# Gate and up of three feed-forwards as seven products of block sums, in an fp32 decoder trunk on one Trainium2 core

## The chip, the cores and the metric

The kernel runs on one core of one Trainium2 chip. The metric is the device time of one execution in microseconds (us), the median of the runs. The engines of the core have names in this text as in the profile: PE is TensorE's matmuls, PEld its loads of the stationary operand, DVE is VectorE, ACT is ScalarE, POOL is GpSimd, SP is SyncE, which here only issues DMAs.

## The reference, cut to what matters

```python
def rms_norm(x, g):
    y = x32 * lax.rsqrt(jnp.mean(x32 * x32, axis=-1, keepdims=True) + NORM_EPS)
    return y * g

def swiglu(x, w_gate, w_up, w_down):
    return (jax.nn.silu(x @ w_gate) * (x @ w_up)) @ w_down

def reference(x, positions, ...):          # x (1, 512, 2048), D_FF = 1536, DEPTH = 2, all float32
    h = x
    for i in range(DEPTH):
        h = h + 0.5 * swiglu(rms_norm(h, norm_g[i, 0]), ffn_w_gate[i, 0], ffn_w_up[i, 0], ffn_w_down[i, 0])
        hn = rms_norm(h, norm_g[i, 1])
        mix = even_mixer(hn, ...) if i % 2 == 0 else odd_mixer(hn, ...)   # attention; pooling and stick-breaking
        h = h + mix
        h = h + 0.5 * swiglu(rms_norm(h, norm_g[i, 2]), ffn_w_gate[i, 1], ffn_w_up[i, 1], ffn_w_down[i, 1])
    return rms_norm(h, final_norm)
```

There are four feed-forwards of 512 positions, 2048 features and 1536 hidden features, and two mixers with their projections between them.

## The kernel before, in words

The activations lie transposed, features on the 128 partitions and the 512 positions along the row: `xg[k]`, k = 0 to 15, is 128 features of all positions. So that fp32 products keep their accuracy, each operand is split in two parts: a high part written as fp32r by an ACT copy, and the rest, `src - high`, by a DVE subtraction. A product of two such pairs is three matmuls (`mm3`: high by high, high by low, low by high) into one PSUM bank. The norm's factor per position, `norm.R`, is multiplied onto the result; its gain is put into `xg` beforehand.

A feed-forward (`ffn`) goes over 12 blocks of 128 hidden features. For each it sums gate into one PSUM bank and up into another, over all 16 k, 48 matmuls each; there the weights' 128 x 128 blocks are stationary and 512 positions move. Then come `gate` (DVE multiply, ACT Silu), `up` (two DVE multiplies) and the split of the result into `hid[f]`. The down projection goes over 16 blocks `d` of 128 output features, 12 k each, 36 matmuls; DVE adds half of it to the residual `x`, and a sink splits the new `x` with the next norm's gain into the next `xg`, squares it on ACT (`Norm.add`, line 329) and adds the square on POOL (line 333). The last down projection does its last four blocks in two halves of positions.

The weights come as a stream of chunks in the order in which PE takes them (`weight_plan`). A chunk is up to 1024 columns of 128 partitions, 512 KB. `load_to` gives the DMA on SP's queue (line 212) into one of 3 raw buffers, `split_to` gives the ACT copy (line 223) and the DVE subtraction (line 224) into one of 3 pairs `wh`, `wl`, and `chunk` does both ahead of the matmuls that use them. The schedule is the order of the program: each engine takes its instructions in the order in which the code gives them, and waits at each for what it needs. Work beside the main stream (heads of attention, rope tables, the last norm) consists of generators in `side`; each call of `tick` gives one more step of one of them.

The norm's sums are closed at the start of the stage that follows, in `Norm.stages`: 4 tiny matmuls with a column of ones (`nps`), a DVE step, a power on POOL, and then, where `bc` is set, 4 transposes (`npb`) that spread the factor over the partitions for `norm.R`. `out_part` is the output projection of a mixer, in two parts by heads, and has the same sink. Residuals of the second and third feed-forward stay in SBUF; around the mixers they are written to DRAM and read back (`spill`, `reload`).

Of the kernel before, what the change touches and what calls it, by code (L numbers as in the profile page):

```python
# [16 lines left out]
P = 128  # L17
S = 512
# [22 lines left out]
DOWN = ((0, NK, 0, S),)  # L41
LAST_DOWN = ((0, NK - 4, 0, S), (NK - 4, NK, 0, S // 2), (NK - 4, NK, S // 2, S))
NRAW = 3
NSPL = 3

# ---------------------------------------------------------------- the order of the weights
# [7 lines left out]
def weight_plan():  # L54
    """(source, layer, half, k0, k1, [(c0, c1), ...]) of each chunk, as TensorE takes them."""
    plan = []
# [8 lines left out]
    def ffn(i, j, first=False, last=False):  # L65
# [10 lines left out]
        for d0, d1, _, _ in LAST_DOWN if last else DOWN:  # L76
            for d in range(d0, d1):
                cols("ffn_w_down", i, j, halves(NF), d * P, d * P + P)
# [18 lines left out]
    for d in range(NK):  # L97
        cols("even_w_out", 0, 0, ((0, A_H),), d * P, d * P + P)
    for d in range(0, NK, 2):
        cols("even_w_out", 0, 0, ((A_H, A_H + B_H),), d * P, d * P + 2 * P)  # L100
    ffn(0, 1)
    ffn(1, 0)
# [9 lines left out]
    for part in range(2):  # L112
        for d in range(0, NK, 2):
            cols("odd_w_out", 0, 0, ((4 * part, 4 * part + 4),), d * P, d * P + 2 * P)
    ffn(1, 1, last=True)
    return plan
# [14 lines left out]
def shape_constants():  # L131
    """Tables that depend on the shapes alone."""
# [38 lines left out]
def trunk(ctx: ExitStack, tc: tile.TileContext, xT, pos_row, pos_col, wts, gains, consts, bias_a_in, bias_b_in, outT):  # L171
    nc = tc.nc
    plan = weight_plan()
# [29 lines left out]
    # ------------------------------------------------------------ the stream of weights  # L203
    nxt_load, nxt_split, nxt_use = [0], [0], [0]
    raw_t, split_t = {}, {}

# [8 lines left out]

    def split_to(i):
        while nxt_split[0] <= min(i, len(plan) - 1):
            j = nxt_split[0]
            n = offsets[j][1]
            r = raw_t.pop(j)  # L220
            h = spl.tile([P, 1024], F32R, tag="wh", name=f"wh_{j}")
            low = spl.tile([P, 1024], F32R, tag="wl", name=f"wl_{j}")
            nc.scalar.activation(h[:, :n], r[:, :n], AF.Copy)  # L223
            nc.vector.tensor_tensor(low[:, :n], r[:, :n], f32(h[:, :n]), op=ALU.subtract)  # L224
            split_t[j] = (h, low)
            nxt_split[0] += 1

    def ahead(i):
        """What may be fetched and split once the products of the chunk before the i-th are given."""
        load_to(i + NRAW + 1)  # L230
        split_to(i + NSPL - 1)

    def chunk(name):
        i = nxt_use[0]
        nxt_use[0] += 1
        assert plan[i][0] == name, (i, plan[i], name)
        ahead(i)
        h, low = split_t.pop(i)
        kk = plan[i][4] - plan[i][3]
        n = offsets[i][1]  # L240
        view = lambda t: t[:, :n].rearrange("p (k c) -> p k c", k=kk)
        return view(h), view(low), range(plan[i][3], plan[i][4])
# [6 lines left out]
    def split(src, s, scale=None, cols=None, late=None):  # L249
        """src (times a column) as two parts of 12 bits; the second one, if late is a list, when its entry is called."""  # L250
# [15 lines left out]
    # ------------------------------------------------------------ work beside the main stream  # L266
# [19 lines left out]
    # ------------------------------------------------------------ constants  # L286
# [123 lines left out]
    # ------------------------------------------------------------ feed-forward  # L410
    def ffn(xg, norm, resid_in, sink, first=False, down=DOWN, beside=None):
# [3 lines left out]
        def half_of(ps, name):  # L415
            wh, wl, ks = chunk(name)
            for i, k in enumerate(ks):
                mm3(ps, wh[:, i, :], wl[:, i, :], xg[k][0], xg[k][1], k == 0, k == NK - 1)
# [14 lines left out]
        if first:  # L433
            pss = [bank("gu") for _ in range(4)]
            for i in range(NK):
                half_of(pss[i % 4], ("ffn_w_gate", "ffn_w_up")[i % 2])
# [26 lines left out]
        for d0, d1, c0, c1 in down:  # L463
            for d in range(d0, d1):
                pd = bank("pd")[:, :c1 - c0]
                for _ in range(2):
                    wh, wl, ks = chunk("ffn_w_down")
                    for i, k in enumerate(ks):
                        mm3(pd, wh[:, i, :], wl[:, i, :], hid[k][0][:, c0:c1], hid[k][1][:, c0:c1], k == 0, k == NF - 1)
                    tick()  # L470
                x = resid_in(d)[:, c0:c1]
                nc.vector.scalar_tensor_tensor(x, pd, 0.5, x, op0=ALU.mult, op1=ALU.add)
                sink(d, x, slice(c0, c1))

    def make_sink(gain, norm, xg, spill=None, keep=None):
        late = []

        def sink(d, x, cols):
# [3 lines left out]
            if d == NK - 1:  # L482
                late.pop()()
            norm.add(x)
            if spill is not None:
                nc.scalar.dma_start(spill[d], x)
            if keep is not None:
                keep[d] = x
# [6 lines left out]
    # ------------------------------------------------------------ attention  # L495
    # Softmax: query blocks; keys and probabilities of blocks in three tiles.
# [4 lines left out]
    def softmax_head(qk, v, bias, scale, merged):  # L501
        """One head: q and k of [features, positions], v of key blocks; the result in merged."""
# [39 lines left out]
    # Stick-breaking: keys on partitions, their queries along the rows, key blocks in three tiles.  # L542
# [65 lines left out]
    # ------------------------------------------------------------ projections  # L608
    def project(name, xg):
        """128 columns of a projection, transposed."""  # L610
        ps = bank("pj")
        for _ in range(2):
            wh, wl, ks = chunk(name)
            for i, k in enumerate(ks):
                mm3(ps, wh[:, i, :], wl[:, i, :], xg[k][0], xg[k][1], k == 0, k == NK - 1)
# [3 lines left out]
    def project_rows(name, xs_of, n, n_chunks, k_last):  # L619
# [352 lines left out]
```

## Time and profile before

| | |
|---|---|
| median of 3 runs | 2329.05 us (2328.59 to 2329.12) |
| span of the profiled execution, first to last instruction | 2327.4 us |
| PE busy | 2307.6 us, 99% of the span |
| DVE, ACT, POOL busy | 1031.5, 769.9, 200.0 us |
| mean granted clock of TensorE | 0.998 of full speed |
| moved by DMA | 243.85 MB, 105 GB/s over the span |

The profile holds the span of its execution and no other time of it; the runs' median is 1.65 us above that span, which is taken as what lies around it. The stages by the profile's time: first feed-forward to 402 us, even mixer with its output to 837, second feed-forward to 1230, third to 1623, odd mixer with its output to 1915, fourth to 2312, last norm to 2327. A matmul's duration in the trace (389 ns) is longer than its distance from the next one, because matmuls overlap; the distance is what counts for time.

### The profile page before, as it was taken

To read this page: it belongs to the slowest core of one execution; us is meant where nothing else is said; L and a number is where in the kernel's file an instruction comes from. 1 tells how busy PE (TensorE), PEld (TensorE's weight loads), DVE (VectorE), ACT (ScalarE), POOL (GpSimd) and SP (SyncE) were. 2 spreads that over 40 slices of the span, in tenths; PEclk is the share of its full clock that TensorE was granted. 3 is DMA by queue.
4 is the path that set the end of the run, shared out by engine and by line. 5 is a ranking of instruction groups with operands and counts; after the bars stand their busy time and mean duration, and the time that the engine had idled before them with its cause. 6 is when DMAs were issued, how large, how long until landed. Compare 5 with 4: busy or idle time off the path is not lost.

```text
span 2327.4 us, 26261 instructions
## 1 busy us (share of the span) xinstructions
PE 2307.6 (99%) x10640; PEld 1937.8 (83%) x10640; DVE 1031.5 (44%) x1350; ACT 769.9 (33%) x1086; POOL 200.0 (9%) x194
## 2 busy tenths in 40 slices
PE   9999999999999999999999999999999999999997
PEld 7888888989888888888888888888888888888887
DVE  4443344464645653333443333344435664333335
ACT  5322233232334442222332222233235553222233
POOL 3000011000011130000110000011300030000013
PEclk9999999999999999999999999999999999999999
DMA  6232334322223332332333332334322422222224
GB/s 210 91 100 91 98 127 136 102 72 97 82 81 128 105 100 91 100 99 82 100 101 98 100 100 91 97 127 138 100 96 82 145 91 100 100 91 100 89 95 161
DMA packets 83530, 243.85 MB, mean 105 GB/s; under 512 B 9296, under 2 KB 13520, under 8 KB 83408
## 3 DMA queue, kind: packets, MB, share of 16 engines
q1 hardware_dynamic: 73328, 224.23, 29.7%
q10 hardware_dynamic: 10080, 17.94, 2.2%
q8 instruction: 83, 1.36, 0.2%
q14 instruction: 39, 0.32, 0.0%
HBM read 229.55 MB, written 12.58 MB: 104 GB/s over the span
## 4 chain that ended last, share of the span: by engine, by line
PE 98%; DVE 0%; DMA 0%; ACT 0%; issue 0%; POOL 0%; DVEq 0%; SPq 0%; ACTq 0%; POOLq 0%
PE pd L246 7%; PE pd L247 7%; PE pd L245 7%; PE pu L245 7%; PE pu L247 7%; PE pg L245 7%; PE pg L247 7%; PE pu L246 7%; PE pg L246 7%; PE pj L245 5%; PE pj L247 5%; PE pj L246 5%; PE wo L245 3%; PE wo L247 3%; PE wo L246 3%; PE pr L245 2%
## 5 line engine op out<-in xcount | busy, mean ns | idle before, releaser
L224 DVE TENSOR_TENSOR wl<-raw,wh 128x1024 fp32r<-128x1024 f32 (+3 forms) x463 | 549.9, 1189 | 755.4 <-ACT wh L223 754.4
L223 ACT ACTIVATE wh<-raw 128x1024 fp32r<-128x1024 f32 (+3 forms) x463 | 443.7, 960 | 609.9 <-issue 185.2
L333 POOL TENSOR_TENSOR sq<-sq,sq 128x512 f32<-128x512 f32 (+1 forms) x110 | 145.4, 1322 | 1916.9 <-ACT sq L329 1915.8
L247 PE MATMUL pd<-hidh,wl 128*128 128x512 f32 (+1 forms) x816 | 307.3, 377 | 0.3 <-DVE wl L224 0.3
L245 PE MATMUL pd<-hidh,wh 128*128 128x512 f32 (+1 forms) x816 | 307.4, 377 | 0.0
L246 PE MATMUL pd<-hidl,wh 128*128 128x512 f32 (+1 forms) x816 | 307.2, 377 | 0.0
L245 PE MATMUL pu<-xgh,wh 128*128 128x512 f32 x736 | 287.0, 390 | 0.0
L245 PE MATMUL pg<-xgh,wh 128*128 128x512 f32 x736 | 286.4, 389 | 0.0
L247 PE MATMUL pu<-xgh,wl 128*128 128x512 f32 x736 | 286.4, 389 | 0.0
L246 PE MATMUL pu<-xgl,wh 128*128 128x512 f32 x736 | 286.4, 389 | 0.0
L247 PE MATMUL pg<-xgh,wl 128*128 128x512 f32 x736 | 286.3, 389 | 0.0
L246 PE MATMUL pg<-xgl,wh 128*128 128x512 f32 x736 | 286.3, 389 | 0.0
L245 PE MATMUL pj<-xgh,wh 128*128 128x512 f32 x464 | 181.7, 392 | 0.0
L247 PE MATMUL pj<-xgh,wl 128*128 128x512 f32 x464 | 180.8, 390 | 0.0
L246 PE MATMUL pj<-xgl,wh 128*128 128x512 f32 x464 | 180.7, 389 | 0.0
L247 PEld LDWEIGHTS pd<-hidh,wl 128*128 128x128 f32 x816 | 153.5, 188 | 28.5 <-DVE wl L224 0.5
L245 PEld LDWEIGHTS pd<-hidh,wh 128*128 128x128 f32 x816 | 153.6, 188 | 28.1
L246 PEld LDWEIGHTS pd<-hidl,wh 128*128 128x128 f32 x816 | 153.6, 188 | 28.1
L247 PEld LDWEIGHTS pu<-xgh,wl 128*128 128x128 f32 x736 | 138.2, 188 | 28.8
L247 PEld LDWEIGHTS pg<-xgh,wl 128*128 128x128 f32 x736 | 138.2, 188 | 28.7
L246 PEld LDWEIGHTS pg<-xgl,wh 128*128 128x128 f32 x736 | 138.2, 188 | 28.7
L246 PEld LDWEIGHTS pu<-xgl,wh 128*128 128x128 f32 x736 | 138.2, 188 | 28.6
(215 smaller groups left out, 2721.1 us busy)
## 6 DMA issues: line engine op xcount, KB each, us to landing
raw<-wts SPq DMA_DIRECT2D x275, 512.0 KB, 3.4
raw<-wts SPq DMA_DIRECT2D x161, 384.0 KB, 3.0
spill<-x ACTq DMA_DIRECT2D x32, 256.0 KB, 2.0
x<-spill ACTq DMA_DIRECT2D x32, 256.0 KB, 2.9
raw<-wts SPq DMA_DIRECT2D x18, 256.0 KB, 2.9
x<-xT SPq DMA_DIRECT2D x16, 256.0 KB, 4.7
outT<-sc SPq DMA_DIRECT2D x16, 256.0 KB, 2.4
raw<-wts SPq DMA_DIRECT2D x8, 416.0 KB, 3.0
```

The costliest lines, as they stand in the source:

```text
L223: nc.scalar.activation(h[:, :n], r[:, :n], AF.Copy)
L224: nc.vector.tensor_tensor(low[:, :n], r[:, :n], f32(h[:, :n]), op=ALU.subtract)
L245: nc.tensor.matmul(out, ah, bh, start=start, stop=False)
L246: nc.tensor.matmul(out, ah, bl, start=False, stop=False)
L247: nc.tensor.matmul(out, al, bh, start=False, stop=stop)
L333: nc.gpsimd.tensor_tensor(self.accs[0], self.accs[0], sq, op=ALU.add)
```

## The change

The second, third and fourth feed-forward compute gate and up by another algorithm (`ffn_products`); the first one, the down projections and the mixers keep theirs.

The 2048 features are two halves (k below and from 8), the 512 positions two halves (256 each), and gate and up of one block of weights are the two columns of a 2 x 2 block matrix. Instead of eight products of blocks there are seven, of sums of blocks (Winograd's form of Strassen's algorithm). Of the inputs, B11, B21, B22 and four sums T1 to T4 are made once per feed-forward and k (`Pieces`): four DVE subtractions of 256 columns and the splits of seven pieces of 256 columns. Of the weights, four sums per block are made in place in the raw buffers by DVE. The products are by position blocks: a 128 x 128 block of a piece is stationary, and 512 hidden features of the weights move. So one unit of 512 hidden features takes 7 products x 8 k x 2 position blocks x 3 matmuls = 336, and 3 units make 1008, beside 1152 before. Units run in two phases, P1, P2 and P4 first (6 PSUM banks), then P6, P5, P7, P3 (8 banks); the results are combined by DVE adds, Silu takes the norm's factor as its scale, and the hidden values, now positions on partitions, are transposed on PE, 16 blocks per unit, and split (`to_hidden`).

For this the stream of weights has a second plan, `uses`: raw chunks of up to 1024 columns in 6 buffers, and splits of at most 512 columns into 4 pairs, everywhere in the kernel. A block of 2 k x 512 columns that is in two products is loaded twice. All sinks write the new residual to DRAM, and the blocks `d` are taken in pairs d, d + 8. The first 5 k of the next pieces are made in `side`, the other three when unit 0 first needs them.

```diff
-NBLK = 81
-NRAW = 3
-NSPL = 3
+NBLK = 79
+NRAW = 6
+NSPL = 4
+LATER = 5
...
+    def ffn_products(i, j, down):              # in the plan of the weights
+        for u in range(FF // UNIT):
+            c0, c1 = u * UNIT, (u + 1) * UNIT
+            blk = lambda name, k: plan.append((name, i, j, k, k + 2, ((c0, c1),)))
+            for k in range(0, HK, 2):
+                blk("ffn_w_up", k)
+                blk("ffn_w_up", HK + k)
+                blk("ffn_w_gate", HK + k)
+            whole()
+            for k in range(0, HK, 2):
+                r = len(plan)
+                a22, a21, a11, a12 = r, r + 1, r + 2, r + 3
+                blk("ffn_w_gate", HK + k)
+                blk("ffn_w_gate", k)
+                blk("ffn_w_up", k)
+                blk("ffn_w_up", HK + k)
+                uses[-3][3].append((a22, a21, 1, a22))
+                uses[-2][3].append((a21, a11, -1, a21))
+                for a, sums in ((a11, [(a11, a22, -1, a11)]), (a22, []), (a21, []), (a12, [(a12, a12, -1, a11)])):
+                    uses.append((a, 0, 1, sums))
+                    uses.append((a, 1, 2, []))
...
     def split_to(i):
-        while nxt_split[0] <= min(i, len(plan) - 1):
+        while nxt_split[0] <= min(i, len(uses) - 1):
             j = nxt_split[0]
+            r, k0, k1, sums = uses[j]
+            load_free()
+            for to, a, sign, b in sums:
+                n = offsets[to][1]
+                nc.vector.tensor_tensor(raw_t[to][:, :n], raw_t[a][:, :n], raw_t[b][:, :n],
+                                        op=ALU.add if sign > 0 else ALU.subtract)
...
+            nc.scalar.activation(h[:, :n], src, AF.Copy)
+            nc.vector.tensor_tensor(low[:, :n], src, f32(h[:, :n]), op=ALU.subtract)
...
+    def take(name, n):
+        while n:
+            i = nxt_use[0]
+            nxt_use[0] += 1
+            r, k0, k1, _ = uses[i]
+            ahead(i)                            # split_to(i + NSPL - 1)
...
+        def steps(self, k, b1, b2):             # Pieces
+            t12, t34 = blk("t12"), blk("t34")
+            sub(t12[:, lo], b1[:, hi], b1[:, lo])
+            sub(t34[:, lo], b2[:, hi], b1[:, hi])
+            sub(t12[:, hi], b2[:, hi], t12[:, lo])
+            sub(t34[:, hi], b2[:, lo], t12[:, hi])
+            yield
+            b = blk("pb", F32R)
+            nc.scalar.activation(b[:, lo], b1[:, lo], AF.Copy)
+            nc.vector.tensor_tensor(b[:, hi], b1[:, lo], f32(b[:, lo]), op=ALU.subtract)
+            b2h, b2l = split(b2, "pb")
+            yield
+            t12h, t12l = split(t12, "pt")
+            yield
+            t34h, t34l = split(t34, "pt")
...
+        def product(names, piece, ps, kc):
+            for k, wh, wl in take(names, 2):
+                k %= HK
+                sh, sl = pieces.get(k)[piece]
+                for a in range(2):
+                    c = slice(a * P, a * P + P)
+                    mm3(ps[a], sh[:, c], sl[:, c], wh, wl, k == 0, k == HK - 1)
...
+        for u in range(FF // UNIT):
+            p1, p2, p4 = ([bank("pa") for _ in both] for _ in range(3))
+            for kc in range(HK // 2):
+                if u == 0 and kc < last:
+                    pieces.get(2 * kc + 2), pieces.get(2 * kc + 3)
+                product("ffn_w_up", "B11", p1, kc)
+                ...                             # kc == last: s1 = copy of p1 (ACT); u == 0, kc < 2: next(ng)
+                tick()
+                product("ffn_w_up", "B21", p2, kc)
+                ...                             # kc == last: c11 = p2 + s1
+                tick()
+                product("ffn_w_gate", "T4", p4, kc)
+                ...                             # kc == last: s4 = copy of p4 (ACT)
+                tick()
+            p6, p5, p7, p3 = ([bank("pb") for _ in both] for _ in range(4))
+            for kc in range(HK // 2):
+                product("ffn_w_up", "T2", p6, kc)
+                if kc == last:
+                    for a in both:
+                        nc.vector.tensor_tensor(s1[a], p6[a], s1[a], op=ALU.add)
+                        nc.vector.tensor_tensor(s4[a], s4[a], s1[a], op=ALU.add)
+                tick()
+                product("ffn_w_gate", "T1", p5, kc)
+                if kc == last:
+                    for a in both:
+                        nc.vector.tensor_tensor(s1[a], p5[a], s1[a], op=ALU.add)
+                tick()
+                product("ffn_w_gate", "T3", p7, kc)
+                if kc == last:
+                    c22 = [blk("c22") for _ in both]
+                    for a in both:
+                        nc.vector.tensor_tensor(s4[a], p7[a], s4[a], op=ALU.add)
+                        nc.scalar.activation(s4[a], s4[a], AF.Silu, scale=norm.r[:, a:a + 1])
+                        nc.vector.tensor_tensor(c22[a], p7[a], s1[a], op=ALU.add)
+                        nc.scalar.activation(c22[a], c22[a], AF.Silu, scale=norm.r[:, 2 + a:3 + a])
+                        nc.vector.scalar_tensor_tensor(c11[a], c11[a], norm.r[:, a:a + 1], s4[a], op0=ALU.mult,
+                                                       op1=ALU.mult)
+                tick()
+                product("ffn_w_up", "B22", p3, kc)
+                tick()
+            for a in both:
+                nc.vector.tensor_tensor(s1[a], p3[a], s1[a], op=ALU.add)
+                nc.vector.scalar_tensor_tensor(s1[a], s1[a], norm.r[:, 2 + a:3 + a], c22[a], op0=ALU.mult, op1=ALU.mult)
+            side.append(to_hidden(u, c11 + s1))
...
+    def piece_sink(gain, norm, pieces, spill):
+        def sink(d, x, cols):
+            b = blk("xb")
+            nc.scalar.activation(b, x, AF.Copy, scale=gain(d))
+            held.append(b)
+            if d >= HK:
+                pieces.add(d - HK, *held)
+                held.clear()
+            norm.add(x)
+            nc.scalar.dma_start(spill[d], x)
```

## Rows read from the trace of the kernel before

**Rows 1.** The page: busy time, chain that ended last, DMA issues (KB, us to landing).
```profile
PE 2307.6 (99%) x10640; PEld 1937.8 (83%) x10640; DVE 1031.5 (44%) x1350; ACT 769.9 (33%) x1086; POOL 200.0 (9%) x194
...
PE 98%; DVE 0%; DMA 0%; ACT 0%; issue 0%; POOL 0%; DVEq 0%; SPq 0%; ACTq 0%; POOLq 0%
...
x<-xT SPq DMA_DIRECT2D x16, 256.0 KB, 4.7
```

**Rows 2.** Stretches (busy us per engine, clock, DMA share, GB/s): start, second feed-forward, end.
```profile
0.00:58.00 58.00, 52.19 (x217) 42.57 (x218) 27.44 (x39) 33.53 (x54) 20.77 (x19) 1.00 0.63 211
...
843.00:1236.00 393.00, 393.00 (x1741) 325.54 (x1740) 154.78 (x165) 113.09 (x141) 23.12 (x18) 1.00 0.31 97
...
2316.00:2327.40 11.40, 0.00 (x0) 0.00 (x0) 6.23 (x5) 0.00 (x0) 5.09 (x4) 0.50 0.66 226
```

**Rows 3.** Timeline of PE and ACT (start us, duration) in the second feed-forward's gate.
```profile
903.97 0.39 PE L245 MATMUL pg<-xgh,wh 128*128 128x512 f32 x1
...
914.39 0.39 PE L246 MATMUL pg<-xgl,wh 128*128 128x512 f32 x1
...
914.85 0.39 PE L245 MATMUL pu<-xgh,wh 128*128 128x512 f32 x1
914.87 1.06 ACT L223 ACTIVATE wh<-raw 128x1024 fp32r<-128x1024 f32 x1 [4.38 <-PE pg L246]
```

**Rows 4.** One tile's matmuls in the odd mixer, where inputs are stationary and weights move.
```profile
L245 PE MATMUL pr<-wh,xgh x9: 389/389/389, 1668.4 to 1673.8; 128*128 128x512 f32 x9
```

**Rows 5.** The chain in order of time (start, us): transposes.
```profile
471.56 1.09 PE pt L528 x10
...
854.70 0.44 PE npb L350 x4
```

**Rows 6.** Timeline of DVE and ACT around one hidden block, second feed-forward.
```profile
904.24 0.69 DVE L428 TENSOR_TENSOR up<-pu,R 128x512 f32<-128x512 f32 x1 [3.37 <-PE pu L247]
...
904.96 0.69 DVE L429 TENSOR_TENSOR gate<-gate,up 128x512 f32<-128x512 f32 x1
...
905.75 0.63 ACT L255 ACTIVATE hidh<-gate 128x512 fp32r<-128x512 f32 x1 [6.14 <-DVE gate L429]
...
906.29 1.05 ACT L223 ACTIVATE wh<-raw 128x1024 fp32r<-128x1024 f32 x1
...
906.49 0.69 DVE L256 TENSOR_TENSOR hidl<-gate,hidh 128x512 fp32r<-128x512 f32 x1 [0.83 <-ACT hidh L255]
```

**Rows 7.** Timeline of DVE, operations one behind the other.
```profile
832.10 0.68 DVE L647 TENSOR_TENSOR x<-wo,x 128x512 f32<-128x512 f32 x1
832.70 0.74 DVE L259 SCALAR_TENSOR_TENSOR xgl<-x,gn,xgh 128x512 fp32r<-128x512 f32 x1
...
1713.80 1.23 DVE L224 TENSOR_TENSOR wl<-raw,wh 128x1024 fp32r<-128x1024 f32 x1 [0.19 <-ACT wh L223]
1714.94 2.72 DVE L259 SCALAR_TENSOR_TENSOR mgcl<-mx,gn,mgch 128x512 fp32r<-128x512 f32 x4
```

**Rows 8.** DMA issues of 512 KB (KB each, median us to landing): second feed-forward's gate and up.
```profile
raw<-wts SPq DMA_DIRECT2D x28, 512.0 KB, 3.6
```

**Rows 9.** Timeline of DVE and POOL at the even mixer's output.
```profile
840.33 3.02 POOL L333 TENSOR_TENSOR sq<-sq,sq 128x512 f32<-128x512 f32 x2 [3.11 <-ACT sq L329]
...
842.43 2.00 DVE L224 TENSOR_TENSOR wl<-raw,wh 128x1024 fp32r<-128x1024 f32 x1 [1.60 <-ACT wh L223]
```

**Rows 10.** The chain in order of time (start, us) at the kernel's start.
```profile
11.23 0.43 PE gu L247
...
12.07 0.24 PE gu L246
```

**Rows 11.** Timeline of PE and POOL after a down projection (third feed-forward starts at 1230.37).
```profile
1230.37 0.39 PE L245 MATMUL pg<-xgh,wh 128*128 128x512 f32 x1
...
1232.74 1.36 POOL L333 TENSOR_TENSOR sq<-sq,sq 128x512 f32<-128x512 f32 x1 [6.87 <-ACT sq L329]
```

**Rows 12.** Timeline of DVE in the softmax of one head, even mixer.
```profile
496.12 0.18 DVE L520 RECIPROCAL rden<-den 128x4 f32<-128x4 f32 x1 [2.36 <-ACT pr L518]
```

More of the change, by code (lines that the diff above doesn't have):

```diff
@@ L54, in weight_plan, with plan_and_uses, whole @@
 def weight_plan():
-    plan = []
+    return plan_and_uses()[0]
+def plan_and_uses():
+    plan, uses = [], []
+    def whole():
+        for r in range(uses[-1][0] + 1 if uses else 0, len(plan)):
+            _, _, _, k0, k1, cs = plan[r]
+            w = sum(b - a for a, b in cs)
+            parts = -(-(k1 - k0) * w // 512)
+            step = -(-(k1 - k0) // parts)
+            for k in range(0, k1 - k0, step):
+                uses.append((r, k, min(k + step, k1 - k0), []))
     def cols(name, i, j, ks, c0, c1):
@@ L63, in halves, with ffn @@
         return ((0, n // 2), (n // 2, n))
-    def ffn(i, j, first=False, last=False):
+    def ffn_products(i, j, down):
[19 more added lines that the diff above has]
+                    uses.append((a, 1, 2, []))
+        for n, (d, _, _) in enumerate(down):
+            if n == 0:
+                for k0, k1 in ((0, 8), (8, NF)):
+                    for e in (down[0][0], down[1][0]):
+                        plan.append(("ffn_w_down", i, j, k0, k1, ((e * P, e * P + P),)))
+            elif n > 1:
+                cols("ffn_w_down", i, j, ((0, 8), (8, NF)), d * P, d * P + P)
+    def ffn(i, j, first=False):
         f = 0
@@ L96, in weight_plan @@
     plan.append(("even_w_kv_up", 0, 0, 0, 2, tuple((h * kvh + NOPE, (h + 1) * kvh) for h in range(B_H))))
[L97 to L102, printed above, removed]
+    for ks in ((0, A_H), (A_H, A_H + B_H)):
+        for d in PAIRS:
+            cols("even_w_out", 0, 0, (ks,), d * P, d * P + P)
+    whole()
+    ffn_products(0, 1, PAIR_DOWN)
+    whole()
+    ffn_products(1, 0, PAIR_DOWN)
     for g in range(4):
@@ L112, in weight_plan @@
     for part in range(2):
[L113 to L116, printed above, removed]
+        for d in PAIRS:
+            cols("odd_w_out", 0, 0, ((4 * part, 4 * part + 4),), d * P, d * P + P)
+    whole()
+    ffn_products(1, 1, LAST_DOWN)
+    whole()
+    return plan, uses
 def plan_offsets(plan):
@@ L205, in trunk @@
     raw_t, split_t = {}, {}
+    last_split = {}
+    for n, (r, _, _, sums) in enumerate(uses):
+        last_split.update({c: n for c in (r, *(x for t, a, _, b in sums for x in (t, a, b)))})
     def load_to(i):
@@ L408, in rope_tables, with ffn, half_of @@
         rope_b["cos"], rope_b["sin"] = cb, sb
-    def ffn(xg, norm, resid_in, sink, first=False, down=DOWN, beside=None):
+    def ffn(xg, norm, resid_in, sink, first=False, beside=None):
         hid = {}
         ng = norm.stages() if norm is not None else None
[L415 to L418, printed above, removed]
+        def half_of(ps, name, n=HK):
+            for k, wh, wl in take(name, n):
+                mm3(ps, wh, wl, xg[k][0], xg[k][1], k == 0, k == NK - 1)
         def gate(ps):
@@ L462, in ffn @@
             tick()
[L463 to L473, printed above, removed]
@@ L475, in make_sink, with down_half, down_done @@
-    def make_sink(gain, norm, xg, spill=None, keep=None):
+        for job in DOWN:
+            pd = bank("pd")
+            for _ in range(2):
+                down_half(pd, job, hid, NF // 2)
+                tick()
+            down_done(pd, job, resid_in, sink)
+    def down_half(pd, job, hid, n):
+        _, c0, c1 = job
+        for k, wh, wl in take("ffn_w_down", n):
+            mm3(pd[:, :c1 - c0], wh, wl, hid[k][0][:, c0:c1], hid[k][1][:, c0:c1], k == 0, k == NF - 1)
+    def down_done(pd, job, resid_in, sink):
+        d, c0, c1 = job
+        x = resid_in(d)[:, c0:c1]
+        nc.vector.scalar_tensor_tensor(x, pd[:, :c1 - c0], 0.5, x, op0=ALU.mult, op1=ALU.add)
+        sink(d, x, slice(c0, c1))
@@ new lines, in trunk, with __init__, add, get @@
+    class Pieces:
+        def __init__(self):
+            self.of, self.work = {}, {}
+        def add(self, k, b1, b2):
+            g = self.steps(k, b1, b2)
+            self.work[k] = g
+            if k < LATER:
+                side.append(g)
+        def steps(self, k, b1, b2):
+            t12, t34 = blk("t12"), blk("t34")
+            lo, hi = slice(0, H), slice(H, S)
+            sub = lambda o, a, b: nc.vector.tensor_tensor(o, a, b, op=ALU.subtract)
+            sub(t12[:, lo], b1[:, hi], b1[:, lo])
[11 more added lines that the diff above has]
+            t34h, t34l = split(t34, "pt")
+            self.of[k] = {
+                "B11": (b[:, lo], b[:, hi]), "B21": (b2h[:, lo], b2l[:, lo]), "B22": (b2h[:, hi], b2l[:, hi]),
+                "T1": (t12h[:, lo], t12l[:, lo]), "T2": (t12h[:, hi], t12l[:, hi]),
+                "T3": (t34h[:, lo], t34l[:, lo]), "T4": (t34h[:, hi], t34l[:, hi])}
+        def get(self, k):
+            if k not in self.of:
+                finish(self.work[k])
+            return self.of[k]
@@ L476, in make_sink @@
+    def make_sink(gain, norm, xg, spill):
         late = []
@@ L703, in trunk @@
     side.append(rope_tables())
-    ffn(xg, norm, lambda d: xs[d], make_sink(g_norm(1), norm1, xg1, spill=spill0), first=True, beside=started)
+    ffn(xg, norm, lambda d: xs[d], make_sink(g_norm(1), norm1, xg1, spill0), first=True, beside=started)
     xs.clear()
```

215 lines of the change are left out of this document (127 added, 88 removed).

## The prediction

> **What bounds the kernel now.** Read the page first: PE is busy 99% of the span, and the chain that ended last is 98% PE [rows 1]. The stretches say that this holds inside a stage too: the second feed-forward has PE busy for 393.0 of 393 us at full clock, DVE 155, ACT 113, DMA share 0.31 [rows 2]. So the time is the number of matmuls times their distance. The timeline gives the distance: 48 matmuls from 903.97 to 914.85, 226.7 ns each [rows 3]. With weights moving and inputs stationary it is the same: nine of every third matmul from 1668.4 to 1673.8, 24 distances in 5.4 us, 225 ns [rows 4]. What leaves PE's stream therefore leaves the time, as long as the engines that feed PE keep up; and they get more to do.
>
> **PE's own account.** Removed: 1152 - 1008 = 144 matmuls in each of three feed-forwards, 432 x 0.2267 = 97.9 us; and the four norm transposes of three norms, 3 x 0.44 = 1.3 [rows 5]. Added: 3 x 48 transposes of 128 x 128; ten took 1.09 us [rows 5], so 144 x 0.109 = 15.7. Without one stall the span would be 2327.4 - 97.9 - 1.3 + 15.7 = 2243.9. No stall at all is the lower end of every term below; the question is how much DVE gives back.
>
> **DVE's prices.** Independent operations of 512 columns follow each other at 0.60 us (832.10 to 832.70, busy 0.68), and 1024 columns take 1.14 (1713.80 to 1714.94) [rows 7]; the line through both gives 256 columns 0.33, an estimate. An operation that reads what the one before it wrote follows after 0.72 (904.24 to 904.96) [rows 6]. A subtraction that waits for an ACT copy of what DVE has just written starts 0.84 after DVE's end (904.96 + 0.69 = 905.65 to 906.49) [rows 6]. One rule speaks against the 0.60: the Trainium skill, VectorE: DVE Perf Modes, section The DRAIN you can't avoid, says that the next operation "does not start until the 8-stage pipe empties", which makes the spacing the whole busy time, 0.69 and 1.23; the same page lets an operation that is not held start earlier, and here the trace decides for 0.60. By the drain rule each group of the second phase below would cost DVE 8 x 0.69 + 4 x 1.23 + 0.84 = 11.3 us against PE's 10.9, and the kernel would come out slower.
>
> **Second phase, steady.** A group is two k of P6, P5, P7, P3: 8 uses of 512 columns, 6 matmuls or 1.36 us each, 10.88 in all. DVE must do 8 subtractions (4.80), 4 sums of 1024 columns (4.56), and waits 0.84 once, after the sum for a11; behind a12's sum another sum stands before the subtraction. That is 10.2 of 10.88. It fits only if the bursts fit in the lead. A pair `wh`, `wl` is free when PE has ended the use four before; ACT starts 0.09 after the last matmul that reads it (914.39 + 0.39 to 914.87 [rows 3]; now that is the third of a block, 0.17 past the next start), copies in 0.63, and DVE follows 0.11 later: 1.0 us after PE's end of use j - 4 subtraction j can start, and PE needs it three uses and one matmul after that end, 4.31. Followed through one group from use 4 on (ready at 2.36, done 2.96; sum 4.10; 4.70; two sums 6.98; 7.58; 8.18; a11's sum 9.32; wait; 10.25; done 10.85, and seen by PE 0.19 later, 11.04), use 0 of the next group is there 0.07 before its second matmul at 11.11. No stall, no reserve.
>
> Into this comes the DMA. a11's buffer comes free when a22's second half is split, at 1.77 on the same clock; a load lands 3.6 us after issue [rows 8], so at about 5.6; DVE needs it for its sum at 5.84. Traffic rises from 97 GB/s to four loads of 512 KB in 10.88 us, 193; the start of the kernel ran 211 GB/s at a DMA share of 0.63 [rows 2], so bandwidth does not bind, but the loads of x landed there in 4.7 us [rows 1]. Ends: 0, and 4.7 - 3.9 = 0.8 us in each of 27 groups that prepare a next one, 22 us. I take 5, nearer to rows 8, because that is the same transfer, mostly alone in flight.
>
> **End of a unit.** Here DVE must do P6's, P5's, P7's and P3's combinations in program order between the splits. From subtraction 0 of the last group (done just in time) to subtraction 9, the second use of what follows: 9 x 0.60 = 5.4, about 0.6 gated, a12's sum 1.14 and a wait of 0.93 with nothing between, P6 4 operations, two dependent, 2.64, P5 1.2, P7 6 operations with two waits for Silu 4.4, ACT's copy behind the last Silu 0.45: done at 16.7, seen at 16.9. PE wants it at 9 x 1.36 + 0.23 = 12.5: 4.4 us of stall. P3's four (2.76) then make use 11 late by another 1.2. So 5.7 us behind units 0 and 1; behind unit 2 the uses are 12 matmuls of the down projection, 2.72 us, and it is 3.1, plus 0.9 for the first transposes that wait for P3's combination. Per feed-forward 2 x 5.7 + 4.0 = 15.4, in three 46. Lower bound, from the amount of work alone (20.5 us of DVE for 14 uses, 19.0 of PE): 1.5 at each of nine ends, 13. Upper: 0.69 in place of 0.60 for some 30 operations, 2.7 more at each, 70. I take 46, since the order is that of the program.
>
> **Pieces.** One k costs DVE 4 x 0.33 + 0.12 + 0.33 + 3 x 0.60 = 3.6 us. Of five k it lies in the stage before, beside 36 matmuls per block (8.2 us) or 12 in a mixer's output (2.7). k = 5 comes at the second pair of k of unit 0, k = 6 and 7 together at the third: subtraction 14 is done at 11 x 1.36 + 1.6 = 16.6, then 7.1 of pieces, subtraction 15 seen at 24.5, wanted at 20.6: 3.9. At the second pair 0.3, or 1.5 where k = 4 has steps left, because a mixer's output gives one tick per block. 4.2 + 2 x 5.4 = 15; between 5, if half of it falls into slack, and 18 by busy times.
>
> **Smaller terms.** The norm's sums were wanted after 48 matmuls and are now wanted after 12, 2.72 us; POOL's last add ended 1234.10 - 1230.37 = 3.7 us after the last down matmul [rows 11]: 1.0 x 3 = 3. In a mixer's output a 1024-column subtraction took 2.00 us beside a POOL add [rows 9] and 1.23 alone [rows 7], 0.77 more; with pieces DVE has about 0.60 + 0.60 + 0.87 + 0.77 = 2.84 for PE's 2.72 per block: 2 us for both outputs, mostly hidden by the lead. (The Trainium skill, SBUF — State Buffer, section Who interferes with whom, names that port: a DVE operation with two SBUF inputs and a POOL operation that reads SBUF block each other. By it the sums and subtractions of the products cost nothing more, since POOL is idle there.) Smaller splits shorten the lead in the mixers from 10.9 to 8.2 us; the longest wait inside a head is 2.36 [rows 12], so I count 1 (0 to 10). Extra instructions on ACT, the writing and reading back of residuals: 0, ACT has under half of its time in use; without that cover they would queue before ACT's copies and lengthen the stalls above.
>
> **Sum.** 2243.9 + 46 + 15 + 5 + 3 + 2 + 1 = 2315.9 of span, plus the 1.65 around it: 2317.6, some 0.5% faster. The gain on PE is 83 us; 72 go back in stalls.
>
> **Rivals.** (1) The stalls stay near their lower bounds: 13 at unit ends, 5 for pieces, 5 for the rest: 2269. For it: DVE's average load in a unit is only some 90%; against it: the order of the program. (2) The clock falls, the other side. At the start PE ran at 0.43 us per matmul up to 11.23 and at 0.24 from 12.07 [rows 10], half and full speed, and in the last 11.4 us without PE the granted clock is 0.50 [rows 2]; in the second feed-forward PE has no idle time that could show more (393.0 of 393 busy, clock 1.00). If each of the nine long stalls (3.3 to 3.9 us at once) lets the clock fall and some 12 matmuls run at 0.43, that is 9 x 12 x 0.2 = 22 us: 2339. It decides as soon as one stall is long enough; by the first rule of the Trainium skill's TensorE: Matmul & The Clock Gate, section HAM oscillation, idle gaps between bursts of matmuls do this. (3) DMA: the late load of every second-phase group costs 1 us instead of 0.2: 27 - 5 more, 2340; for it the knife's edge above, against it the DMA share. (4) DVE holds PE everywhere in the second phase (drain spacing): 0.4 x 36 + 24 at unit ends, 2350.
>
> **Chances and range.** Forecast (2306 to 2331) 0.50, rival (1) 0.20, (2) 0.12, (3) 0.12, (4) 0.06. A measurement of this kernel can tell about 0.2% from no change, 4.7 us. The forecast lies two thirds below 2324.4, a quarter within, the rest above; (1) is faster, (2) to (4) are slower but for a tenth: faster 0.54, same 0.15, slower 0.31. The range goes from just above (1) to just beyond (4), 2268 to 2352.
>
> **What would show it.** Right: PE busy down by about 83 us; gaps of PE behind each unit's last product that end with the DVE subtraction of line `split_to`; one of about 4 us at the third pair of k in unit 0; DVE busy above 85% in second phases. Wrong: gaps in every group that end with a DMA (3); 0.43 us matmuls behind gaps (2); no PE gap above 2 us (1); DVE operations spaced at their busy time (4).

## The result, and the profile of the changed kernel

The changed kernel takes 2392.86 us (median of 4 runs, 2391.04 to 2394.99), the kernel before beside it 2329.09: a ratio of 1.0275, 95% interval 1.026 to 1.0289. It is 2.75% slower; the forecast was 2317.6, 0.5% faster, and the range ended at 2352. The forecast was wrong in sign and in size.

The page of the changed kernel has, against [rows 1], a PE that is no longer busy throughout, and a tenth of the chain on DVE:

```profile
PE 2283.9 (95%) x10340; PEld 1886.3 (79%) x10340; DVE 1474.4 (62%) x2300; ACT 1017.2 (43%) x1823; POOL 188.0 (8%) x194
...
PE 83%; DVE 10%; ACT 4%; issue 2%; DMA 1%; POOL 0%; DVEq 0%; ACTq 0%; SPq 0%; POOLq 0%
```

The count of matmuls is the forecast one (10640 - 432 + 144 - 12 = 10340). What PE waited for (us in total, times, longest):

```profile
PE pa L323 <- ACT wh L295: 27.5, 11, 3.8
PE nps L418 <- POOL sq L411: 25.0, 3, 12.6
...
PE wo L323 <- ACT wh L295: 9.7, 9, 1.3
PE pa L324 <- DVE wl L296: 8.7, 13, 1.0
PE wo L325 <- DVE wl L296: 7.6, 11, 0.7
```

`wo` is a mixer's output, where the forecast had next to nothing, and `nps` the norm's sums, which it had at 1.0 us each. The stretches put both in place (columns as in [rows 2]); in order: output of the even mixer, first half of unit 0 behind it, a second half; first half of unit 0 of the third feed-forward, which follows no mixer; that whole feed-forward; the odd mixer's output and the unit 0 behind it.

```profile
795.00:854.40 59.40, 51.33 (x195) 38.69 (x194) 35.08 (x52) 26.95 (x48) 13.96 (x11) 0.91 0.43 137
854.40:915.30 60.90, 41.02 (x154) 31.55 (x152) 43.97 (x74) 31.94 (x59) 6.37 (x6) 0.83 0.38 121
...
915.30:960.20 44.90, 44.53 (x194) 35.74 (x193) 39.83 (x54) 18.17 (x33) 0.00 (x0) 1.00 0.56 178
...
1266.00:1307.30 41.30, 37.52 (x154) 29.67 (x153) 30.66 (x53) 22.62 (x41) 2.68 (x2) 0.92 0.45 147
...
1266.00:1655.90 389.90, 378.30 (x1642) 306.54 (x1641) 277.99 (x385) 173.80 (x296) 20.77 (x16) 0.98 0.52 168
...
1904.10:1963.20 59.10, 49.93 (x194) 37.29 (x194) 34.87 (x52) 26.96 (x48) 13.72 (x11) 0.95 0.42 138
1963.20:2023.90 60.70, 42.22 (x153) 32.05 (x152) 44.16 (x74) 31.92 (x59) 6.58 (x6) 0.77 0.38 122
```

An output's second part is 192 matmuls, 43.5 us at 0.2267; it takes 59.4, though DVE is busy for only 35.1 of them. Unit 0's first half is 144 matmuls and 8 small ones, 33.4 us; it takes 60.9 behind a mixer and 41.3 in the third feed-forward. That feed-forward as a whole takes 389.9 us, where before its 393.3 us (1236.0 to 1629.3) were all PE.

This table has the time lost in each place, that is the distances between the starts of matmuls less 0.2267 per matmul (a matmul at half clock counts as loss too); the last four columns are experiments below.

| place | forecast | changed | 7 pairs alone | late sinks and norms | with spread pieces | with 7 pairs too |
|---|---|---|---|---|---|---|
| outputs of two mixers | 2 | 15.8, 15.6 | 0.7, 0.6 | 0, 0 | 0, 0 | 0, 0 |
| unit 0 behind them, first half | 6.4, 6.4 | 27.5, 27.2 | 35.2, 34.3 | 12.9, 14.5 | 8.7, 8.7 | 6.4, 6.3 |
| unit 0 of the third, first half | 5.2 | 7.9 | 1.2 | 5.0 | 2.3 | 0.2 |
| first halves of the six later units | 34 | 34 | 9.5 | 32 | 32 | 7.3 |
| nine second halves | 5 | 14 | 3.5 | 13 | 16 | 4 |

The miss of the span is 2393.0 - 2315.9 = 77 us, and the first two rows have 86.1 - 14.8 = 71 of it.

**What happens there.** The timeline of the changed kernel in the even mixer's output, about one block, and its end (start, duration, engine, line; in brackets the idle time before and what ended it):

```profile
802.18 0.68 DVE L874 TENSOR_TENSOR x<-wo,x 128x512 f32<-128x512 f32 x1
...
816.78 0.68 DVE L874 TENSOR_TENSOR x<-wo,x 128x512 f32<-128x512 f32 x1
...
817.49 0.72 ACT L718 ACTIVATE xb<-x,gn 128x512 f32<-128x512 f32 x1 [2.18 <-DVE x L874]
...
818.12 0.62 ACT L407 ACTIVATE sq<-x 128x512 f32<-128x512 f32 x1
818.64 0.62 ACT L295 ACTIVATE wh<-raw 128x512 fp32r<-128x512 f32 x1
...
818.88 1.29 POOL L411 TENSOR_TENSOR sq<-sq,sq 128x512 f32<-128x512 f32 x1 [3.17 <-ACT sq L407]
...
819.29 1.42 DVE L296 TENSOR_TENSOR wl<-raw,wh 128x512 fp32r<-128x512 f32 x1 [1.83 <-ACT wh L295]
...
822.09 0.68 DVE L874 TENSOR_TENSOR x<-wo,x 128x512 f32<-128x512 f32 x1
...
870.20 0.68 DVE L874 TENSOR_TENSOR x<-wo,x 128x512 f32<-128x512 f32 x1
872.35 1.27 POOL L411 TENSOR_TENSOR sq<-sq,sq 128x512 f32<-128x512 f32 x1 [3.23 <-ACT sq L407]
873.68 1.87 PE L418 MATMUL nps<-ones,sq 128*128 128x1 f32 x8 [12.64 <-POOL sq L411]
```

Read it as a ring. The addition `x` lets ACT go on with `xb` and `sq` of the sink; only behind these stands the copy `wh` of the block that comes some blocks later; DVE's next instruction in program order is the subtraction `wl` of that copy, for which it idles 1.83 us and which takes 1.42 in place of 0.69 because it meets POOL's addition; behind it come a step of the pieces and then the next `x`, although its PSUM bank has long been summed. From 802.18 to 870.20 there are 14 such rounds, 4.86 us each, against 2.72 us of PE per block. So the splits come late (`wo` waits), and the last `x` comes 16 us after PE has left the output at 854.4; the square sums end with it, and PE waits 12.6 us for them.

The kernel before had this ring too, though a faster one, with one split for two blocks:

```profile
801.45 0.68 DVE L647 TENSOR_TENSOR x<-wo,x 128x512 f32<-128x512 f32 x1
...
844.36 0.68 DVE L647 TENSOR_TENSOR x<-wo,x 128x512 f32<-128x512 f32 x1
```

Between these rows lie 7 rounds of two blocks, 6.13 us each, so 3.07 per block, already slower than PE's 2.72, and the last addition came 7 us after PE's last matmul of the output (837.04 + 0.23). It cost PE nothing in that output (43.60 us busy of the 43.60 from 793.7 to 837.3). That three pairs of 1024 columns and a norm that was first wanted after 48 matmuls are what hid it is read from the order of the program; no run of before tests it.

### The profile page after: what moved, and what is told of

It is laid out like the page before. It is cut to its first block, busy times and chain, and to the rows that moved or that the text cites. A ratio compares the mean times of both kernels' runs of the same rounds, so it can differ in the third digit from the quotient of the medians.

```text
span 2393.0 us, 28548 instructions
## 1 busy us (share of the span) xinstructions
PE 2283.9 (95%) x10340; PEld 1886.3 (79%) x10340; DVE 1474.4 (62%) x2300; ACT 1017.2 (43%) x1823; POOL 188.0 (8%) x194
## 4 chain that ended last, share of the span: by engine, by line
PE 83%; DVE 10%; ACT 4%; issue 2%; DMA 1%; POOL 0%; DVEq 0%; ACTq 0%; SPq 0%; POOLq 0%
PE pd L323 7%; PE pd L325 7%; PE pd L324 7%; PE pj L323 4%; PE pj L325 4%; PE pj L324 4%; PE pb L324 4%; PE pa L324 4%; DVE wl L296 4%; PE pb L325 4%; PE pb L323 4%; PE pa L323 3%; PE pa L325 3%; PE wo L325 2%; PE wo L323 2%; PE wo L324 2%
## 5 line engine op out<-in xcount | busy, mean ns | idle before, releaser
L296 DVE TENSOR_TENSOR wl<-raw,wh 128x512 fp32r<-128x512 f32 (+2 forms) x1071 | 755.9, 729 | 636.5 <-ACT wh L295 625.8
L295 ACT ACTIVATE wh<-raw 128x512 fp32r<-128x512 f32 (+2 forms) x1071 | 631.4, 613 | 788.1 <-DVE raw L288 180.5
L288 DVE TENSOR_TENSOR raw<-raw,raw 128x1024 f32<-128x1024 f32 x144 | 174.1, 1218 | 6.1 <-DMA raw<-wts 5.8
L324 PE MATMUL pb<-wl,pth 128*128 128x512 f32 x432 | 169.0, 391 | 0.7 <-DVE wl L296 0.7
L323 PE MATMUL pb<-wh,pth 128*128 128x512 f32 x432 | 168.1, 389 | 0.0
L325 PE MATMUL pb<-wh,ptl 128*128 128x512 f32 x432 | 168.1, 389 | 0.0
L323 PE MATMUL wo<-mgh,wh 128*128 128x512 f32 x224 | 92.5, 413 | 9.7 <-ACT wh L295 9.7
L324 PEld LDWEIGHTS pj<-xgl,wh 128*128 128x128 f32 x464 | 87.2, 188 | 17.4
L323 PEld LDWEIGHTS pj<-xgh,wh 128*128 128x128 f32 x464 | 87.2, 188 | 17.3
L325 PE MATMUL wo<-mgh,wl 128*128 128x512 f32 x224 | 92.3, 412 | 7.6 <-DVE wl L296 7.6
```

Source lines behind the costliest of these rows:

```text
L288: nc.vector.tensor_tensor(raw_t[to][:, :n], raw_t[a][:, :n], raw_t[b][:, :n], op=ALU.add if sign > 0 else ALU.subtract)
L295: nc.scalar.activation(h[:, :n], src, AF.Copy)
L296: nc.vector.tensor_tensor(low[:, :n], src, f32(h[:, :n]), op=ALU.subtract)
L323: nc.tensor.matmul(out, ah, bh, start=start, stop=False)
L324: nc.tensor.matmul(out, ah, bl, start=False, stop=False)
L325: nc.tensor.matmul(out, al, bh, start=False, stop=stop)
```

## Experiments

Theory A is that ring. Its rivals are in the expectations. Each kernel has its ratio to the kernel before, measured beside it.

**Late sinks.** Each sink of an output is given one block later, so that ACT's copy of the next weights no longer stands behind a sink that waits for DVE.

```diff
+        held = None
...
             nc.vector.tensor_tensor(x, po, x, op=ALU.add)
-            sink(d, x, None)
+            if held is not None:
+                sink(*held)
+            held = (d, x, None)
+        sink(*held)
```

> The sink of the mixers' output projections (scaled copy, square, write to DRAM, pieces) is given one block later, behind the next block's split and add; nothing is left out. Theory A, a ring: in the second part of each mixer's output the chain DVE add of x, ACT scaled copy, ACT square, ACT copy of the next weights, DVE subtraction of them (held up by POOL), step of a piece, next DVE add goes round once per block in some 4.85 us, where PE needs 2.72; the lateness, some 34 us at each of two outputs, is paid partly there (15.7 us) and partly in unit 0 of the next feed-forward (27 us beside 8 us in the third feed-forward, which follows no mixer). With the sink late the ring spans two blocks: outputs lose 1 to 5 us instead of 15.7, unit 0 8 to 12 instead of 27, together 45 to 65 us less: 2328 to 2348. Theory B, the wait for the norm's sums is the cost by itself (PE waits 25 us for POOL's last add in all, and the clock falls behind it): the sums become complete about as late as before, less than 15 us gained: 2378 to 2393.

2341.89 us, ratio 1.0055 (1.004 to 1.007): 51.0 us gained by order alone. DVE of this kernel in the same output:

```profile
800.62 0.68 DVE L875 TENSOR_TENSOR x<-wo,x 128x512 f32<-128x512 f32 x1
...
837.41 0.68 DVE L875 TENSOR_TENSOR x<-wo,x 128x512 f32<-128x512 f32 x1
838.01 1.18 DVE L296 TENSOR_TENSOR wl<-raw,wh 128x512 fp32r<-128x512 f32 x1
...
843.80 0.68 DVE L875 TENSOR_TENSOR x<-wo,x 128x512 f32<-128x512 f32 x1
...
DVE wl L296 <- ACT wh L295: 5.6, 4, 1.5
```

The last line is DVE's waits from 797 to 841; in the changed kernel, from 797 to 871, that line is 28.9 us in 16 times. The 14 rounds from 800.62 to 843.80 take 3.08 us each, which is near the 2.84 of work that the forecast had and short enough for the lead: the outputs lose nothing. The time is inside A's interval and far from B's. The units 0 behind the outputs still lose 17.5 and 17.7, more than the 8 to 12 expected.

**Late norms.** The norm's stages begin after the third pair of k instead of the first.

```diff
-                if u == 0 and kc < 2:
+                if u == 0 and kc >= 2:
                     next(ng, None)
```

> The norm's sums are closed behind the third and fourth pair of k of unit 0 instead of the first and second; nothing else is changed or left out. Theory A: the wait for POOL is only the place where the late sinks are noticed; PE then waits in unit 0 for splits and pieces that stand behind the same sinks on DVE: 0 to 10 us gained, 2383 to 2393. Theory B: the 25 us of waiting and some 10 us of half clock behind them go: 2355 to 2365.

2381.73 us, ratio 1.0225 (1.021 to 1.024): 11.1 us gained, 1.3 more than A's bound and far from B's. No wait of `nps` for POOL is left, and the time goes over to the next one in the ring's wake (waits of this kernel):

```profile
PE pa L323 <- ACT wh L295: 33.4, 18, 3.8
PE pa L324 <- DVE wl L296: 12.6, 19, 1.0
PE wo L323 <- ACT wh L295: 10.5, 11, 1.3
PE wo L325 <- DVE wl L296: 9.0, 13, 0.7
```

So the 25 us at `nps` were mostly the place where the ring's delay was seen, not its cause.

**Both.**

> Both edits, late sinks in the mixers' outputs and late closing of the norm's sums. Theory A: 3 to 10 us below the kernel with the late sinks alone, since 1 us and the fall of the clock at the start of three feed-forwards go: 2320 to 2342. Theory B: the same as the kernel with the norm late alone, within 15 us.

2332.82 us, ratio 1.0016 (1.0007 to 1.0026): 60.0 us, the two gains nearly added up (62.1). It is 9.1 below the kernel with late sinks, as A had it, and 49 below the one with late norms, which B had within 15.

**No square sums on POOL.** The additions of squares are left out for the three norms ahead of the products.

```diff
-            else:
+            elif self.n != DM or self.bc:
                 nc.gpsimd...
```

> Leaves out POOL's adds of squares in the three norms in front of the seven-product feed-forwards, so that their factor is taken from one block of features instead of sixteen. Theory A: the subtraction of the weights takes 0.69 instead of 1.42 us in the mixers' outputs, the ring is 0.73 shorter, 16 blocks, two outputs: 23 us less, 2365 to 2372, with the rest of the lateness still there. Theory B: the wait for the sums goes as a whole, 25 to 35 us: 2355 to 2368; a large overlap with A, so this run prices POOL's hold on DVE and decides little else.

2362.99 us, ratio 1.0145 (1.013 to 1.016): 2 us below A's interval, so this run by its time does not tell the theories apart; the timeline of this kernel does:

```profile
814.52 0.68 DVE L874 TENSOR_TENSOR x<-wo,x 128x512 f32<-128x512 f32 x1
817.04 0.69 DVE L296 TENSOR_TENSOR wl<-raw,wh 128x512 fp32r<-128x512 f32 x1 [1.83 <-ACT wh L295]
...
819.12 0.68 DVE L874 TENSOR_TENSOR x<-wo,x 128x512 f32<-128x512 f32 x1
```

DVE's wait for ACT stays 1.83, the subtraction is back at 0.69, and the rounds are 4.13 us (14 from 802.08 to 859.94). POOL's hold is thus 0.73 of each round's 4.86, over 16 blocks and two outputs 23 of the 30 us gained. Each output still loses 7.9.

**Seven pairs alone.** The changed kernel with 7 pairs `wh`, `wl` instead of 4 (and 6 fewer common blocks, which pays for them).

```diff
-NBLK = 79
+NBLK = 73
...
-NSPL = 4
+NSPL = 7
```

> The changed kernel with seven pairs of buffers for the weights' parts in place of four, and nothing else: the sinks of the mixers' outputs and the norms stay in the changed kernel's order. Theory A (ring): a longer lead lets TensorE run further ahead of the ring in the outputs, but the ring (addition, two copies of ScalarE, the next subtraction) still takes its 4.85 us per block, so the last sums of squares come as late as before and the first unit behind takes back what the output gains: output and first unit together still lose 75 to 90 us over the two mixers. Only the losses that are no ring's go, as they went from the run with late sinks and norms to the one with seven pairs: unit ends and second phases in all three feed-forwards, the third one's first unit. That is 30 to 45 us: 2345 to 2365 us. Theory F (the lead alone decides, and the ring is only what a short lead looks like): the time falls to within 20 us of the run with seven pairs, late sinks and spread pieces, 2278 to 2300 us.

2338.78 us, ratio 1.0042 (1.0025 to 1.0059). F is refuted. A's interval is missed by 6 us on the fast side; its sum for output and unit 0 was 75 to 90 and is 70.8. The ring itself did not move (additions, waits, then the stretches of output and unit 0 behind it):

```profile
805.57 0.68 DVE L874 TENSOR_TENSOR x<-wo,x 128x512 f32<-128x512 f32 x1
...
873.52 0.68 DVE L874 TENSOR_TENSOR x<-wo,x 128x512 f32<-128x512 f32 x1
...
PE nps L418 <- POOL sq L411: 52.7, 3, 26.0
...
798.40:842.70 44.30, 43.79 (x195) 35.98 (x193) 25.55 (x39) 19.97 (x36) 9.56 (x8) 1.00 0.46 149
842.70:911.30 68.60, 39.77 (x153) 31.00 (x154) 50.89 (x83) 35.24 (x67) 10.73 (x9) 0.73 0.37 118
```

14 rounds take 67.95 us, 4.85 each, as with 4 pairs. PE runs ahead of the ring through the whole output, loses 0.7 us there, and then waits 26 us for the sums. More buffers move the wait; they don't speed up the ring. Of the 54 us gained, 15 are at the outputs and the units behind them and the rest in the other rows of the table.

**Six pairs, on top of late sinks and norms** (`NSPL = 6`, `NBLK = 75`):

> On top of late sinks and late closing of the norm's sums: 6 pairs of split weights instead of 4 (and 75 blocks of activations instead of 79), so that splits run two uses, 2.7 us, further ahead; nothing left out. Theory C, bursts: the 4.7 to 7.2 us lost in the first phase of units 1 and 2 and the 1 to 2.4 in each second phase come from DVE's combinations, sums and waits in program order, longer than the lead, while DVE's average load leaves room; each burst then costs 2.7 us less: 16 at unit ends, some 10 in second phases, 5 at the down projections, 8 in first units: 2290 to 2305. Rival D, throughput: DVE has no reserve in the second phase, so more lead only moves the stall to a later place: less than 10 us gained, 2322 to 2333.

2298.05 us, ratio 0.9868 (0.9853 to 0.9882): C, and 34.8 us gained. The ends of units shrink, from 5.0 to about 2.2 us at the third unit of each feed-forward.

**Spread pieces, on top of late sinks and norms.** Two steps of the pieces ahead of each product of unit 0's first half, instead of all steps of two k at once.

```diff
-                if u == 0 and kc < last:
-                    pieces.get(2 * kc + 2), pieces.get(2 * kc + 3)
+                steps(u, 2)
                 product("ffn_w_up", "B11", p1, kc)
...                                             # the same line ahead of B21 and of T4
```

> On top of late sinks and late closing of the norm's sums, with 4 pairs: the pieces of k = 2 to 7 are made in unit 0 by two steps ahead of each product of the first phase instead of whole at the second and third pair of k; nothing left out. Theory C: the burst of two pieces, 7.1 us of DVE, is what costs 5.0 us in unit 0 of the third feed-forward and part of 12.9 and 14.5 us in the second and fourth; without it 0 to 1 in the third and 6 to 10 in the others: 10 to 18 us less, 2315 to 2323. Rival D: the work is the same and DVE has no reserve: within 5 us of 2333.

2319.36 us, ratio 0.996 (0.9946 to 0.9975): 13.5 us, as C said of the time. The rows of unit 0 in the table fall by 4.2, 5.8 and 2.7; the third feed-forward's still loses 2.3, where C had 0 to 1, and the second halves lose more than without the spread, 16 for 13.

**Both of these, with six and with seven pairs.**

> Both: 6 pairs and pieces spread over the first phase. Theory C: 2280 to 2300, below both the kernel before and the changed one. Rival D: 2315 to 2333.

> 7 pairs (and 73 blocks of activations) with pieces spread. Theory C: another 1.36 us per burst that is left: 5 to 12 us below the one with 6 pairs, 2270 to 2292. Rival D: the same as with 6 pairs within 3 us; fewer blocks of activations could make DVE and ACT wait for free ones and take some of it back.

2294.93 us, ratio 0.9859 (0.9843 to 0.9876), and 2278.32 us, ratio 0.9783 (0.9769 to 0.9798). With six pairs the spread adds 3 us only: without it the third feed-forward's unit 0 already lost no more than 0.4. The seventh pair gains 16.6, more than the 5 to 12 expected, with the time inside C's interval. 11 of them are at ends of units: the first halves of the six later units lost 2.3 to 5.4 us each with six pairs, and four of them 0.2 with seven. Stretches of the kernel with seven pairs: unit 0 behind the even mixer, then the first and the second half of the third feed-forward's second unit:

```profile
840.90:880.70 39.80, 36.00 (x154) 27.25 (x152) 37.05 (x66) 24.88 (x49) 7.07 (x5) 1.00 0.47 150
1296.90:1331.40 34.50, 34.50 (x161) 28.57 (x160) 29.00 (x44) 20.99 (x37) 0.00 (x0) 1.00 0.56 177
1331.40:1374.90 43.50, 43.50 (x193) 36.03 (x192) 38.48 (x52) 18.89 (x33) 0.00 (x0) 1.00 0.63 198
```

This version beats both kernels, the one before by 2.2%. PE is busy without a gap in the last two stretches; 12.7 us are still lost in the two units behind the mixers.

## Why the prediction was wrong

**The step that failed** is the term "2 us for both outputs, mostly hidden by the lead". It compared DVE's busy time per block, 2.84 us, with PE's 2.72. It left out that DVE stands still until ACT has the copy ready: 2.84 + 1.83 is 4.67, and the rounds measured 4.86. So the outputs and the first halves behind them lost 86 us where the forecast had 15. The operations and the POOL hold were priced about right; the loop they form, through two engines that each work in program order, was not followed once round. The trace of before had it in sight, with additions 3.07 us per block against 2.72.

**Norm sums, 1.0 each**, failed for the same reason: the 3.7 us of [rows 11] belong to a down projection, whose sums end soon after PE. In the third feed-forward, behind a down projection, the wait was 0.8; behind the mixers it was 12.6 and 11.6 (25.0 in all).

**Pieces** were right in place and size where nothing else was late: in the third feed-forward the stall at the third pair of k came as forecast, about 4 us, and that unit 0 lost 7.9 in all against 5.2; of the 2.7 more, 2.2 are eleven matmuls at half speed right behind the stall. Behind the mixers the pieces came on top: with late sinks and norms those halves lost 12.9 and 14.5 instead of 6.4, of which spreading the pieces took 4.2 and 5.8. What the rest is, these runs leave open.

**Ends of units** were right in place, and 34 us in six first halves by the forecast and by the trace; that the sums agree so well is partly luck. Up to 8 of the measured 34 are matmuls at half speed, and at two of the six ends ACT loads a table for Silu (1.28 us each, at 960.16 and 2068.43), where PE's longest wait is 3.8 us instead of 2.4 or 2.5; the forecast had neither. The down projections lost 2.4 at their start, against 4.0.

**Second halves** were under-sized, 14 for 5, but the 5 was a price for late loads alone, and that price was about right. In the changed kernel DVE waited 5.8 us for `raw` loads, 8 times in all. The five halves in which these waits sum to 0.6 us or more lost 1.4 to 2.8 us, the other four 1.0 to 1.1. The longest such wait, and PE's wait for the next split behind it:

```profile
1008.61 1.23 DVE L288 TENSOR_TENSOR raw<-raw,raw 128x1024 f32<-128x1024 f32 x1 [1.90 <-DMA raw<-wts]
...
1010.49 0.50 PE L324 MATMUL pb<-wl,pbh 128*128 128x512 f32 x1 [1.02 <-DVE wl L296]
```

The other 9 us are 1.0 in the last group of each half, where splits stand behind P6's and P5's combinations; the forecast took this group's splits as just in time. DVE's share in such a half is 89% (39.83 of 44.90), as forecast.

**The feed-forward by itself**: for the third, 393.3 - 144 x 0.2267 - 0.4 + 48 x 0.109 = 365.5 without a stall; with its share of the forecast stalls (5.2 + 15.4 + 1.7) 387.8, measured 389.9. The change does about what was forecast where no mixer's output precedes it. It gains 3 us there, so the other losses decide.

**The signs.** The stall at the third pair of k and DVE above 85% in second phases came, and so did a sign against the forecast, matmuls at 0.43 us behind gaps. PE's busy time fell by 23.7 us (2307.6 to 2283.9) and not by 83; some 25 us of the difference are matmuls at half speed, and the rest is not traced. The longest waits at the ends of units end with ACT's copy `wh` and not with the DVE subtraction.

**Rivals.** (4) did not happen: DVE's operations follow each other at 0.60 (837.41 to 838.01 in the kernel with late sinks). Its own terms added to the forecast give 2356, not 2350, 4 us beyond the end of the range. (3) did not happen at its size: late loads held DVE 8 times, where it had one in each of 27 groups, and none of PE's waits listed for the changed kernel ends with a DMA. (1) did not happen in the changed kernel; with late sinks, late norms, spread pieces and seven pairs together the time comes within 10 us of it (2278.32 for 2269). (2) did happen, and at about its price: the changed kernel has 134 matmuls at half speed and the one before 11, and by the distances of the starts the difference is 25 us, where (2) had 108 matmuls and 22. How much of this is time is known in a few places only, as the last section shows. It is not what set the ring: the kernel with seven pairs alone has its output at clock 1.00 and the same rounds.

## What to carry to other kernels

Price a stage not only by each engine's busy time per block but by its rings: follow one block through all engines in program order until the same instruction comes again, add waits and hand-overs, and compare that with the bounding engine's time per block. A ring that is longer than that is hidden as long as a lead lasts and someone downstream is not yet waiting; a change that shortens the lead and wants the result earlier uncovers it. The cure that took no buffers here was to give the sink one block later. More buffers covered bursts of work (the ends of units) but moved most of the ring's wait downstream: output and first half behind it lost 86.1 us with four pairs and 70.8 with seven.

## What the runs showed of the hardware

The clock. PE of the changed kernel behind its 12.6 us wait, and later (starts and durations):

```profile
876.41 0.63 PE L325 MATMUL pa<-wh,pbl 128*128 128x512 f32 x1
876.83 0.63 PE L323 MATMUL pa<-wh,pbh 128*128 128x512 f32 x1
...
886.12 0.39 PE L324 MATMUL pa<-wl,pb 128*128 128x512 f32 x1
886.35 0.39 PE L325 MATMUL pa<-wh,pb 128*128 128x512 f32 x1
```

Matmuls start 0.43 us apart, half speed (1.2 GHz), and 0.23 apart in the later rows (2.4 GHz); 13 matmuls in a row ran at half speed. Behind eight of nine shorter stalls, with 2.7 to 4.2 us from one start to the next, 4 to 12 matmuls did so too; behind the ninth none. What this cost differs. The same half of a third unit, once with such a fall and once without, in the kernel with late sinks and norms:

```profile
1016.70:1056.10 39.40, 36.73 (x162) 29.61 (x161) 28.46 (x42) 21.84 (x37) 0.00 (x0) 0.96 0.54 171
2091.60:2130.70 39.10, 35.46 (x161) 28.43 (x160) 28.50 (x42) 21.90 (x37) 0.00 (x0) 1.00 0.52 173
```

They differ by 0.3 us, where PE at half speed has spent 1.4 us more on its matmuls and 1.1 us less on waiting (by the distances of the starts). But the third feed-forward's second unit, first half, in the changed kernel (12 matmuls at half speed) and in the one with late sinks (4):

```profile
1352.40:1392.90 40.50, 37.99 (x162) 30.49 (x161) 28.52 (x42) 21.89 (x37) 0.00 (x0) 0.92 0.55 168
...
1325.90:1365.00 39.10, 36.60 (x162) 29.44 (x161) 28.47 (x42) 21.91 (x37) 0.00 (x0) 0.96 0.54 174
```

Here nearly all of the 1.6 us that eight more matmuls at half speed take is lost, 1.4. How much the clock adds in the first unit behind a mixer these runs don't tell.

DVE and POOL. A 512-column subtraction took 1.42 us beside a POOL addition and 0.69 in the kernel without these additions, 0.73 less; the forecast had 0.77. The Trainium skill, SBUF — State Buffer, section Who interferes with whom, says that a DVE operation with two SBUF inputs contends with a POOL operation that reads SBUF. The trace agrees: 1.42 us beside such an operation, 0.69 without. What had not been expected is how far it reaches: inside the ring each such hold was paid in full, 0.73 us a round and 23 us in all, though DVE idles for 40% of the stretch.
